# Convolution taps turned behind the first gate block, and block copies split by the partitions they write

## The chip, the cores and the metric

The kernel runs on one core of one Trainium2 chip. The metric is the device time of one launch in microseconds (us). Engines are named as the profile names them: PE is TensorE, DVE is VectorE, ACT is ScalarE, POOL is GpSimd, SP is SyncE.

## What is computed

An encoder trunk of two layers over 256 tokens of width 2048, in float32. Each layer is a token mixer followed by a gated MLP, with RMS normalisation in front and a residual add behind; the change touches only the MLP:

```python
def conv_ffn(h, w_up, conv_w, conv_b, w_down):
    u = h @ w_up                       # 2048 -> 2 * 5632
    u = conv over positions, width 3, one filter per channel (u, conv_w) + conv_b
    gate, val = jnp.split(u, 2, axis=-1)
    return (jax.nn.silu(gate) * val) @ w_down

for i in range(2):
    h = h + mixer_i(rms_norm(h, mix_norm[i]))
    h = h + conv_ffn(rms_norm(h, ffn_norm[i]), w_up[i], conv_w[i], conv_b[i], w_down[i])
return rms_norm(h, final_norm)
```

## The kernel before

Every large product is a stream of PE matmuls of 128x128 by 128x512. Weights arrive from HBM as `raw` tiles (128x1024 floats, half of a 512-row group) through SP's DMA queue, six buffers in turn. ACT rounds each to `wh` (line 126), DVE subtracts to get the rest `wl` (line 127), and PE multiplies three times: high by high, high by `wl`, low by high (lines 151 to 153). The pair `wh`, `wl` has three buffers in turn, so ACT begins a split when PE has left the buffers of three splits ago. One split feeds twelve matmuls. The two lines are built at a raised priority, so that the scheduler puts them ahead of other work in the queues of ACT and DVE; otherwise each engine does its instructions in one fixed order.

In the MLP the up-projection is done in 22 output blocks of 512 channels per layer, a gate block and its value block in turn (11 pairs, 6 in the first half and 5 in the second; behind each half stands its part of the down-projection, lines 259 to 264). A block is 96 matmuls, eight splits. When its sums are complete, the generator `up_post` is started, which goes on a step at a time while PE works on the next block:

- ACT scales the sums out of PSUM to `s` (line 426), and DVE transposes 32x32 squares from `s` to `t` (line 427). This turns the squares, but leaves them in the wrong partitions.
- Sixteen copies move them from `t` to `u`, each from 32 partitions to 32 partitions. Copy `i` reads partition group `a = i // 4` and writes group `b = (i // 4 + i) % 4`; within `u` the columns that different `a` write interleave. `PLACE` (line 26) names the engine of each: `p` POOL (line 436), `a` ACT (line 438), anything else DVE (line 440). Before, the sixteen letters go by `i`: five for POOL, three for ACT, eight for DVE, and every group `b` is written by several engines.
- ACT and DVE do the convolution with the taps `cw` (lines 446, 450, 452), ACT the silu (455), DVE the product with the value block (460 or 468), and both engines the split of the result for the down-projection (276, 277). Part of the down-projection uses seven products in place of eight, for which DVE also adds activations (484 to 496) and weights (line 228).

The framework adds semaphore waits between instructions that touch the same tile in overlapping places. It takes two copies to the same partitions with interleaving columns as overlapping.

The taps lie in HBM by row. Two DMAs on POOL's queue bring them to `cr` (lines 392, 393), and `taps()` turns them: three PE transposes into one PSUM bank (line 399) and a DVE copy to `cw` (line 400). `taps_gen` is started before the first block and runs when `step()` next reaches it, which is in the first splits of the first gate block. That block and its value block are done by `project2`: three of four row groups of the gate, three of the value, then `drain()`, the last group of the gate, `first_done` (which starts `up_post` of the gate), and the last group of the value.

In layer 0 there is one more piece of side work in the MLP, `bias_lines`: six PE products, each copied by DVE to one of two halves of `lnt` (line 890) and sent to HBM by four DMAs on POOL's queue (line 894).

Of the kernel before, what the change touches and what calls it, by code (L numbers as in the profile page):

```python
# [18 lines left out]
NPAIR = 11  # L19
# [3 lines left out]
NRAW, NHL = 6, 3  # L23
SKG = ((0, 2), (0,))
ORDER = (1, 2, 5, 3, 7, 6, 4)
PLACE = "pvavpvpvavpvpvav"
AHEAD = 45
NWARM = 11

# [2 lines left out]
def tile_encoder(ctx: ExitStack, tc: tile.TileContext, x, xT, w_a, w_ao, q_gain, k_gain, w_b, w_bo,  # L32
# [34 lines left out]
    def ps_tile():  # L67
        bank_at[1] = (bank_at[1] + 1) % 4
        return bank(4 + bank_at[1], "ps")
# [12 lines left out]
    def start(gen):  # L82
        if next(gen, StopIteration) is not StopIteration:
            pending.append(gen)
# [15 lines left out]
    def drain(keep=0):  # L100
        while len(pending) > keep:
            step()
# [34 lines left out]
    def feed(accs, lhs, kg, wap, first, last, by_m=False, pieces=2, mid=None):  # L137
        raws = [new_raw(), new_raw()]
        for i in range(pieces):
            w = 2048 // pieces  # L140
            r = raws[2 * i // pieces].rearrange("p a c -> p (a c)")
            o = i * w % 1024
            nc.sync.dma_start(r[:, o:o + w], wap[:, i * w:(i + 1) * w])
            if mid is not None:
                mid(i)
        def mms(order):
            for m, kt in order:
                (wh, wl), j = hls[kt // 2], kt % 2
                xh, xl = at(lhs[4 * kg + kt], m)
                st, sp = first and kt == 0, last and kt == 3  # L150
                nc.tensor.matmul(accs[m], xh, wh[:, j, :], start=st, stop=False)  # L151
                nc.tensor.matmul(accs[m], xh, wl[:, j, :], start=False, stop=False)  # L152
                nc.tensor.matmul(accs[m], xl, wh[:, j, :], start=False, stop=sp)  # L153

        hls = []
        for s in range(2):
            r = raws[s]
            if pieces == 4:
                wh, wl = new_hl()
                with tc.high_priority(offset=AHEAD):  # L160
                    for i in range(2):
                        nc.scalar.activation(wh[:, i], r[:, i], AF.Copy)  # L162
                        nc.vector.tensor_tensor(wl[:, i], r[:, i], wh[:, i].bitcast(F32), ALU.subtract)
                done_raw(r)
                hls.append((wh, wl))
            else:
                hls.append(split_raw(r))
            if not by_m:
                mms([(m, kt) for kt in (2 * s, 2 * s + 1) for m in range(2)])
                step()  # L170
        if by_m:
            mms([(m, kt) for m in range(2) for kt in range(4)])

    def new_acc():
        bank_at[0] = (bank_at[0] + 2) % 4
        return [bank(bank_at[0] + m, "acc") for m in range(2)]
# [8 lines left out]
    def project2(w, n0, n1, lhs, kgs, late, first_done, hook=None):  # L185
        a0, a1 = new_acc(), new_acc()
        early = len(kgs) - late
        for k, part in enumerate((range(early), range(early, len(kgs)))):
            if k == 1:
                drain()  # L190
            for accs, n in ((a0, n0), (a1, n1)):
                for i in part:
                    kg = kgs[i]
                    mid = hook and hook(n == n0, kg)
                    feed(accs, lhs, kg, w[n, kg], i == 0, i == len(kgs) - 1,
                         pieces=4 if hook and i < 2 else 2, mid=mid)
                if k == 1 and n == n0:
                    first_done(a0)
        return a1
# [182 lines left out]
    def ffn(l, hT, ss_in, g_next, last, side=None):  # L382
        with tc.tile_pool(name=nm("wpool"), bufs=1) as wp, tc.tile_pool(name=nm("fpool"), bufs=1) as fp:
# [11 lines left out]
            def taps():  # L395
                t = ps_tile()
                for a in range(3):
                    w = min(P, NROW - a * P)
                    nc.tensor.transpose(t[:, a * P:a * P + w], cr[:w, a, :], ident[:w, :w])
                nc.vector.tensor_copy(cw, t[:, :NROW])  # L400
# [6 lines left out]
            for u in us:  # L407
                nc.gpsimd.memset(u[:, :, P:P + 1], 0.0)

            def taps_gen():  # L410
                yield
                taps()

            start(taps_gen())

            def halves(v):
                return v.rearrange("p (m t) -> p m t", m=2)

            def up_post(acc, n, cs, after=None):
                u = us.pop(0)  # L420
                us.append(u)
                yield
                s = fp.tile([P, 2, 512], F32, tag="s", name=nm("s"))
                t = fp.tile([P, 2, 512], F32, tag="t", name=nm("t"))
                for m in range(2):
                    nc.scalar.activation(s[:, m], acc[m], AF.Copy, scale=rstd[:, m:m + 1])
                    nc.vector.transpose(t[:, m], s[:, m])  # L427
                yield
                tv = t.rearrange("p m (j q c) -> p j m q c", j=4, q=4)
                uv = u.rearrange("p j (m t) -> p j m t", m=2)  # L430
                for i in range(16):
                    a, b = i // 4, (i // 4 + i) % 4
                    dst = uv[32 * b:32 * b + 32, :, :, 32 * a:32 * a + 32]
                    src = tv[32 * a:32 * a + 32, :, :, b]
                    if PLACE[i] == "p":
                        nc.gpsimd.tensor_copy(dst, src)  # L436
                    elif PLACE[i] == "a":
                        nc.scalar.activation(dst, src, AF.Copy)  # L438
                    else:
                        nc.vector.tensor_copy(dst, src)  # L440
                yield
                for hh in range(2):
                    yield
                    c = cs[hh]
                    for j in range(2):
                        nc.scalar.activation(halves(c[:, j]), halves(u[:, 2 * hh + j])[:, :, :P], AF.Identity,
                                             bias=tap(n, 2 * hh + j, 3), scale=tap(n, 2 * hh + j, 1))
                    for j in range(2):
                        cj, uj = halves(c[:, j]), u[:, 2 * hh + j]
                        nc.vector.scalar_tensor_tensor(cj, halves(uj[:, :NT])[:, ::-1], tap(n, 2 * hh + j, 0), cj,  # L450
                                                       ALU.mult, ALU.add)
                        nc.vector.scalar_tensor_tensor(cj, halves(uj[:, 1:NT + 1])[:, ::-1], tap(n, 2 * hh + j, 2), cj,
                                                       ALU.mult, ALU.add)
                    if after is None:
                        nc.scalar.activation(c, c, AF.Silu)
                    else:
                        yield from after(hh)
# [43 lines left out]
            kgs = list(range(4))  # L501
            for hf, (p0, p1) in enumerate(HALVES):
# [8 lines left out]
                for p in range(p0, p1):  # L511
                    if p - p0 in SKG[hf]:
                        fm = forms[p - p0] = {f: new_form() for f in (1, 7, 2, 5, 4, 6, 3) + (0,) * hf}
                        if hf:
                            for kt in range(4):
                                slots[4 * (p - p0) + kt] = [
                                    tuple(t[:, kt % 2 * P:(kt % 2 + 1) * P] for t in fm[f])
                                    for f in ((1, 0), (2, 4))[kt // 2]]
                    else:
                        slots.update({4 * (p - p0) + j: new_form() for j in range(4)})  # L520
                    cg, cv = ([fp.tile([P, 2, NT], F32, tag=t, name=nm(t), bufs=3) for _ in range(2)]
                              for t in ("cg", "cv"))

                    def after(hh, cg=cg, cv=cv, slots=slots, forms=forms, kg=p - p0):
                        if kg in forms:
                            return glu_forms(cg[hh], cv[hh], forms[kg], hh)
                        return glu(cg[hh], cv[hh], slots, 4 * kg + 2 * hh)

                    if p == 0:
                        va = project2(w_up[l], p, NPAIR + p, hT, kgs, 1,  # L530
                                      lambda a, cg=cg: start(up_post(a, 0, cg)))
                    else:
                        start(up_post(project(w_up[l], p, hT, kgs), p, cg))
                        va = project(w_up[l], NPAIR + p, hT, kgs)
                    start(up_post(va, NPAIR + p, cv, after))
                    if p == 1 and side is not None:
                        spare.append(side(wp, fp))
# [491 lines left out]
    hT, ss = mixer_a()  # L1029
    hT, ss = ffn(0, hT, ss, 2, False, bias_lines)  # L1030
    hT, ss = mixer_b(hT, ss)
# [85 lines left out]
```

## Time and profile before

| | |
|---|---|
| median of 3 runs | 2297.68 us (2296.09 to 2298.33) |
| profiled execution, time | 2300.27 us |
| its span, first to last instruction | 2298.5 us |
| PE busy | 2263.6 us (98%) |
| DVE busy | 1808.1 us (79%) |
| ACT busy | 1296.6 us (56%) |
| POOL busy | 227.5 us (10%) |
| HBM traffic over the span | 189 GB/s |

A time in the trace is counted from the start of the span. A row of the timeline gives start, duration, engine, line, operation, and in brackets the idle time before it and what ended it. Matmuls overlap, each shown at about 0.39 us though the next begins sooner, so what PE loses is read from the distance between starts. Rows of several windows give for each stretch the busy time of each engine with its count, and the clock that PE was granted.

### The profile page before, as it was taken

What the parts mean: (1) busy time and instruction counts of PE and PEld (TensorE: products, weight loads), DVE (VectorE), ACT (ScalarE), POOL (GpSimd) and SP (SyncE); (2) the same over time, 40 slices, a digit from 0 to 9 for tenths busy, and PEclk for the clock granted to TensorE, in tenths of its full rate; (3) what the DMA queues carried; (4) which work ended last, traced back from release to release, by engine and by line L of the source; (5) the groups of instructions that cost most, each with busy time, mean ns of one, the idle gap of its engine ahead of it and who ended that gap; (6) DMA issues with size and microseconds to landing.
All of it is one profiled execution on the core that took longest, in us unless ns stands there. A gap on an engine that the chain in (4) does not pass through costs nothing.

```text
span 2298.5 us, 28788 instructions
## 1 busy us (share of the span) xinstructions
PE 2263.6 (98%) x10169; PEld 1863.5 (81%) x10169; DVE 1808.1 (79%) x2697; ACT 1296.6 (56%) x1846; POOL 227.5 (10%) x328
## 2 busy tenths in 40 slices
PE   9999899999999999999999999999999999999998
PEld 7788688787888888888888888877788878888876
DVE  6877778888978888978776876584988888788884
ACT  6565456666546666555554554454766655466653
POOL 2210012211001111010000000000211100111110
PEclk9999999999999999999999999999999999999999
DMA  8445557765666565666655565555556566656663
GB/s 300 151 144 156 177 168 210 224 196 170 217 209 189 191 197 163 214 223 196 197 177 171 181 191 164 177 185 191 184 191 193 187 200 209 192 184 196 208 209 128
DMA packets 126449, 437.42 MB, mean 190 GB/s; under 512 B 17264, under 2 KB 18032, under 8 KB 126304
## 3 DMA queue, kind: packets, MB, share of 16 engines
q1 hardware_dynamic: 119744, 425.64, 57.8%
q0 software_dynamic: 6128, 9.38, 1.6%
q8 instruction: 79, 1.29, 0.2%
q14 instruction: 66, 0.54, 0.1%
q10 hardware_dynamic: 432, 0.56, 0.1%
HBM read 429.20 MB, written 6.29 MB: 189 GB/s over the span
## 4 chain that ended last, share of the span: by engine, by line
PE 80%; DVE 13%; issue 3%; DMA 2%; ACT 1%; POOL 1%; SPq 0%; DVEq 0%; POOLq 0%; ACTq 0%
PE acc L152 21%; PE acc L153 21%; PE acc L151 21%; DVE wl L127 6%; PE acc L264 5%; PE acc L261 4%; PE acc L259 4%; DVE tT L320 1%; DVE u L440 1%; ACT wh L126 1%; DMA scr<-lnt 1%; DVE al L277 1%; DVE cv L450 1%; PE ps L291 1%; DVE t L427 1%
## 5 line engine op out<-in xcount | busy, mean ns | idle before, releaser
L127 DVE TENSOR_TENSOR wl<-raw,wh 128x1024 fp32r<-128x1024 f32 x822 | 1001.4, 1225 | 318.1 <-ACT wh L126 313.4
L126 ACT ACTIVATE wh<-raw 128x1024 fp32r<-128x1024 f32 x822 | 863.8, 1057 | 630.0 <-PE acc L153 403.8
L152 PE MATMUL acc<-wl,xh 128*128 128x512 f32 x2176 | 853.0, 392 | 6.3 <-DVE wl L127 5.5
L151 PE MATMUL acc<-wh,xh 128*128 128x512 f32 x2176 | 854.2, 393 | 0.1
L153 PE MATMUL acc<-wh,xh 128*128 128x512 f32 x2176 | 850.3, 391 | 0.0
L152 PEld LDWEIGHTS acc<-wl,xh 128*128 128x128 f32 x2176 | 409.8, 188 | 99.3 <-DVE wl L127 15.6
L153 PEld LDWEIGHTS acc<-wh,xh 128*128 128x128 f32 x2176 | 409.9, 188 | 84.4
L151 PEld LDWEIGHTS acc<-wh,xh 128*128 128x128 f32 x2176 | 409.8, 188 | 83.8 <-ACT wh L162 0.6
L436 POOL COPY u<-t 32x256 f32<-32x256 f32 x220 | 141.2, 642 | 1044.1 <-DVE t L427 1016.2
L259 PE MATMUL acc<-wh,ah 128*128 128x512 f32 x524 | 204.2, 390 | 0.0
L261 PE MATMUL acc<-wh,al 128*128 128x512 f32 x524 | 204.2, 390 | 0.0
L152 PE MATMUL acc<-wl,ah 128*128 128x512 f32 x480 | 188.2, 392 | 2.0 <-DVE wl L127 1.8
L151 PE MATMUL acc<-wh,ah 128*128 128x512 f32 x480 | 187.6, 391 | 0.0
L153 PE MATMUL acc<-wh,al 128*128 128x512 f32 x480 | 187.3, 390 | 0.0
L264 PE MATMUL acc<-wl,ah 128*128 128x512 f32 x524 | 147.0, 392 | 5.8 <-DVE wl L127 5.5
L440 DVE COPY u<-t 32x256 f32<-32x256 f32 x352 | 125.6, 357 | 15.7 <-ACT u L438 5.7
L264 PEld LDWEIGHTS acc<-wl,ah 128*128 128x128 f32 x524 | 97.6, 188 | 29.5 <-DVE wl L127 9.6
L259 PEld LDWEIGHTS acc<-wh,ah 128*128 128x128 f32 x524 | 98.5, 188 | 20.5
L261 PEld LDWEIGHTS acc<-wh,al 128*128 128x128 f32 x524 | 98.4, 188 | 20.5
L438 ACT ACTIVATE u<-t 32x256 f32<-32x256 f32 x132 | 55.2, 418 | 97.9 <-DVE u L440 85.6
L152 PEld LDWEIGHTS acc<-wl,ah 128*128 128x128 f32 x480 | 90.2, 188 | 23.9 <-DVE wl L127 5.8
L151 PEld LDWEIGHTS acc<-wh,ah 128*128 128x128 f32 x480 | 90.2, 188 | 18.3
(170 smaller groups left out, 1622.9 us busy)
## 6 DMA issues: line engine op xcount, KB each, us to landing
raw<-in_w_up_dram SPq DMA_DIRECT2D x352, 512.0 KB, 4.4
raw<-in_w_down_dram SPq DMA_DIRECT2D x176, 512.0 KB, 4.6
raw<-in_w_b_dram SPq DMA_DIRECT2D x144, 512.0 KB, 4.0
raw<-in_w_bo_dram SPq DMA_DIRECT2D x48, 512.0 KB, 4.0
raw<-in_w_a_dram SPq DMA_DIRECT2D x40, 512.0 KB, 4.8
raw<-in_w_ao_dram SPq DMA_DIRECT2D x32, 512.0 KB, 4.0
raw<-in_w_a_dram SPq DMA_DIRECT2D x16, 256.0 KB, 6.3
h<-in_x_dram SPq DMA_DIRECT2D x4, 512.0 KB, 9.1
```

What stands on the lines that cost most here:

```text
L126: nc.scalar.activation(wh, r, AF.Copy)
L127: nc.vector.tensor_tensor(wl, r, wh.bitcast(F32), ALU.subtract)
L151: nc.tensor.matmul(accs[m], xh, wh[:, j, :], start=st, stop=False)
L152: nc.tensor.matmul(accs[m], xh, wl[:, j, :], start=False, stop=False)
L153: nc.tensor.matmul(accs[m], xl, wh[:, j, :], start=False, stop=sp)
L259: nc.tensor.matmul(acc[k], xh, wh[:, j, :], start=k in fresh, stop=False)
L261: nc.tensor.matmul(acc[k], xl, wh[:, j, :], start=False, stop=False)
L264: nc.tensor.matmul(acc[k], xh, wl[:, j, :], start=False, stop=last[k] == i and j == 1)
L277: nc.vector.tensor_tensor(lo, src, hi.bitcast(F32), ALU.subtract)
L436: nc.gpsimd.tensor_copy(dst, src)
L438: nc.scalar.activation(dst, src, AF.Copy)
L440: nc.vector.tensor_copy(dst, src)
```

## The change

Two edits. First, `taps()` is no longer a generator of its own; it is called when the first gate block is complete, in front of that block's `up_post`. The two DMAs to `cr` stay where they were. Second, `PLACE` has four letters and is read by the written group `b`: group 0 is written by POOL, groups 1 and 3 by ACT, group 2 by DVE. So of the sixteen copies of a block POOL has four (five before), ACT eight (three) and DVE four (eight); there are 44 blocks in all.

```diff
-PLACE = "pvavpvpvavpvpvav"
+PLACE = "pava"
...
             for u in us:
                 nc.gpsimd.memset(u[:, :, P:P + 1], 0.0)
 
-            def taps_gen():
-                yield
-                taps()
-
-            start(taps_gen())
-
             def halves(v):
...
-                    if PLACE[i] == "p":
+                    if PLACE[b] == "p":
                         nc.gpsimd.tensor_copy(dst, src)
-                    elif PLACE[i] == "a":
+                    elif PLACE[b] == "a":
                         nc.scalar.activation(dst, src, AF.Copy)
                     else:
                         nc.vector.tensor_copy(dst, src)
...
                     if p == 0:
-                        va = project2(w_up[l], p, NPAIR + p, hT, kgs, 1,
-                                      lambda a, cg=cg: start(up_post(a, 0, cg)))
+                        def gate_done(a, cg=cg):
+                            taps()
+                            start(up_post(a, 0, cg))
+
+                        va = project2(w_up[l], p, NPAIR + p, hT, kgs, 1, gate_done)
```

Lines behind line 409 move up by six in the changed kernel, and lines behind line 531 by three, so the copies stand there at 430 (POOL), 432 (ACT) and 434 (DVE).

Nothing else moves on PE, and SP's order is unchanged. PE's queue in layer 0, at the second split of the first gate block, before (`acc_2629` is the gate's second half, `xh_2296` the last input slice of the first row group, `h` is transposed for later input slices):

```order
L151 MATMUL acc_2629<-wh_2657,xh_2296 128x512
L399 MATMUL ps_2652<-ident,cr_2603 128x128 x2
L152 MATMUL acc_2629<-wl_2658,xh_2296 128x512
L399 MATMUL ps_2652<-ident,cr_2603 128x96
L153 MATMUL acc_2629<-wh_2657,xh_2296 128x512
L347 MATMUL ps_2673<-ident,h 128x128 x4
```

The three transposes of the taps stood in the middle of a group of matmuls. After the change they stand behind the last matmul of the gate block, in front of the value block's last row group (`acc_2630`):

```order
L152 MATMUL acc_2629<-wl_2891,xh_2707 128x512
L153 MATMUL acc_2629<-wh_2890,xh_2707 128x512
L399 MATMUL ps_2906<-ident,cr_2603 128x128 x2
L399 MATMUL ps_2906<-ident,cr_2603 128x96
L151 MATMUL acc_2630<-wh_2915,xh_2673 128x512
L152 MATMUL acc_2630<-wl_2916,xh_2673 128x512
```

They moved by 146 matmuls; layer 1 has the same move.

ACT's queue for a block in the middle of layer 0, before, with the engines whose semaphores a row waits on (`t_4445` is the block's transposed tile, `u_2606` its destination):

```order
L426 ACTIVATE s_4444<-acc_4233,rstd_2597 128x512
L126 ACTIVATE wh_4502<-raw_4483 128x1024 [waits DMAHW2_49,DVE_49,PE_49]
L438 ACTIVATE u_2606<-t_4445 32x8x32 [waits DVE_49] x3
L126 ACTIVATE wh_4529<-raw_4525 128x1024 [waits DMAHW3_49,PE_49]
```

and after:

```order
L420 ACTIVATE s_4444<-acc_4233,rstd_2597 128x512
L126 ACTIVATE wh_4502<-raw_4483 128x1024 [waits DMAHW2_49,DVE_49,PE_49]
L432 ACTIVATE u_2606<-t_4445 32x8x32 [waits DVE_49]
L432 ACTIVATE u_2606<-t_4445 32x8x32
L432 ACTIVATE u_2606<-t_4445 32x8x32 [waits Activation_49] x4
L126 ACTIVATE wh_4529<-raw_4525 128x1024 [waits DMAHW3_49,PE_49]
L432 ACTIVATE u_2606<-t_4445 32x8x32 [waits Activation_49]
L432 ACTIVATE u_2606<-t_4445 32x8x32
```

Only the first copy waits for another engine, and six copies instead of three stand in front of the next weight split.

DVE's queue for the same block, before:

```order
L427 STREAM_TRANSPOSE t_4445<-s_4444 128x512 [waits Activation_49]
L440 COPY u_2606<-t_4445 32x8x32 [waits DVE_49]
L440 COPY u_2606<-t_4445 32x8x32
L440 COPY u_2606<-t_4445 32x8x32 [waits Pool_49] x3
L127 TENSOR_TENSOR wl_4503<-raw_4483,wh_4502 128x1024 [waits DMAHW2_49,Activation_49]
L440 COPY u_2606<-t_4445 32x8x32 [waits Activation_49]
L440 COPY u_2606<-t_4445 32x8x32 [waits Pool_49]
L440 COPY u_2606<-t_4445 32x8x32 [waits Activation_49]
```

and after:

```order
L421 STREAM_TRANSPOSE t_4445<-s_4444 128x512 [waits Activation_49]
L434 COPY u_2606<-t_4445 32x8x32 [waits DVE_49] x3
L127 TENSOR_TENSOR wl_4503<-raw_4483,wh_4502 128x1024 [waits DMAHW2_49,Activation_49]
L434 COPY u_2606<-t_4445 32x8x32 [waits DVE_49]
L127 TENSOR_TENSOR wl_4530<-raw_4525,wh_4529 128x1024 [waits DMAHW3_49,Activation_49]
```

DVE's copies no longer wait for POOL or ACT, and three instead of five stand in front of the next subtraction. Each copy waits for the copy before it on its own engine.

## The prediction

> **What bounds the kernel now.** I read the page first, then windows over the MLP, then PE's timeline where they show a loss, and last the queues of ACT and DVE. The page gives PE, and the copies by engine:
>
> ```profile
> PE 2263.6 (98%) x10169; PEld 1863.5 (81%) x10169; DVE 1808.1 (79%) x2697; ACT 1296.6 (56%) x1846; POOL 227.5 (10%) x328
> L436 POOL COPY u<-t 32x256 f32<-32x256 f32 x220 | 141.2, 642 | 1044.1 <-DVE t L427 1016.2
> L440 DVE COPY u<-t 32x256 f32<-32x256 f32 x352 | 125.6, 357 | 15.7 <-ACT u L438 5.7
> L438 ACT ACTIVATE u<-t 32x256 f32<-32x256 f32 x132 | 55.2, 418 | 97.9 <-DVE u L440 85.6
> ```
>
> PE is the bound almost everywhere, so a change off PE counts only where PE stands still. The windows (length, then busy us and count of PE, PEld, DVE, ACT, POOL, then PE's clock) say where that is:
>
> ```profile
> 279.00:286.00 7.00, 5.38 (x16) 4.38 (x17) 3.10 (x5) 1.90 (x3) 0.00 (x0) 0.52 0.27 95
> 316.00:372.00 56.00, 55.06 (x241) 44.56 (x240) 52.62 (x92) 41.31 (x62) 10.76 (x17) 1.00 0.60 185
> 372.00:428.00 56.00, 54.09 (x225) 42.94 (x224) 42.75 (x72) 30.75 (x46) 22.33 (x35) 0.97 0.77 232
> 428.00:550.00 122.00, 121.99 (x538) 100.76 (x537) 104.36 (x169) 79.31 (x116) 17.89 (x29) 1.00 0.64 200
> 550.00:583.00 33.00, 31.68 (x138) 25.50 (x138) 31.52 (x44) 20.71 (x28) 3.26 (x5) 1.00 0.48 152
> 905.00:930.00 25.00, 23.06 (x100) 18.06 (x99) 24.88 (x34) 15.90 (x22) 1.65 (x2) 1.00 0.52 175
> 1608.00:1665.00 57.00, 56.10 (x245) 45.42 (x244) 53.53 (x95) 42.01 (x63) 11.81 (x20) 1.00 0.60 185
> 1840.00:1870.00 30.00, 28.68 (x125) 23.03 (x124) 27.34 (x39) 18.08 (x24) 2.70 (x5) 1.00 0.56 188
> 2190.00:2215.00 25.00, 23.77 (x104) 18.98 (x104) 25.00 (x33) 15.37 (x20) 0.00 (x0) 1.00 0.66 203
> ```
>
> In the middle of an up-projection (428 to 550) PE is never idle: 122.00 / 538 = 0.227 us for each matmul, my pitch below. It is idle where the up-projection begins (316, 1608) and where the down-projection begins (550, 905, 1840, 2190), and there DVE is full: 31.52 of 33, 25.00 of 25. The largest loss is in front of these, in the first gate block. PE's timeline in layer 0, then layer 1, with the two DMA issues of layer 0 on POOL:
>
> ```profile
> 273.98 0.39 PE L151 MATMUL acc<-wh,xh 128*128 128x512 f32 x1
> 277.14 0.41 PE L399 MATMUL ps<-ident,cr 128*128 128x128 f32 x2 [2.77 <-POOL rb L877]
> 280.62 0.42 PE L399 MATMUL ps<-ident,cr 96*128 96x96 f32 x1 [2.83 <-DMA cr<-in_conv_dram]
> ...
> 285.58 0.47 PE L153 MATMUL acc<-wh,xh 128*128 128x512 f32 x1
> 285.89 0.39 PE L151 MATMUL acc<-wh,xh 128*128 128x512 f32 x1
> 1570.67 0.39 PE L151 MATMUL acc<-wh,xh 128*128 128x512 f32 x1
> 1573.51 0.41 PE L399 MATMUL ps<-ident,cr 128*128 128x128 f32 x2 [2.45 <-issue]
> 1574.98 0.60 PE L347 MATMUL ps<-ident,h 128*128 128x128 f32 x4
> 1575.34 0.48 PE L151 MATMUL acc<-wh,xh 128*128 128x512 f32 x1
> 1575.65 0.40 PE L152 MATMUL acc<-wl,xh 128*128 128x512 f32 x1
> 272.64 0.79 POOL L392 DMA_DIRECT2D cr<-in_conv_dram  x1 [94.07 <-DMA raw<-in_w_up_dram]
> 275.01 0.57 POOL L393 DMA_DIRECT2D cr<-in_conv_dram  x1
> ```
>
> The taps' transposes stand in PE's queue a microsecond or two behind the issue of the DMAs that feed them, and the whole queue waits for the landing, once for each DMA.
>
> **The taps.** Layer 0: from 273.98 to 285.89 are 11.91 us. Twelve 512-wide matmuls begin in it: 12 x 0.227 = 2.72. The four transposes of `h` cost 0.36 (1574.98 to 1575.34), and the matmul behind them 0.31 in place of 0.227: 0.44 together. So 8.75 us are lost, of which some 2 are no wait: behind it PE ran at clock 0.52 (window 279 to 286). Layer 1: from 1570.67 to 1575.65 are 4.98, less four matmuls (0.91) and 0.44: 3.63. At the new place the same three transposes cost three quarters of 0.44 again, 0.33 for each layer, and no wait: their DMAs were issued at 272.64 and 275.01, some 40 us before. DVE's copy to `cw` stands in front of one `wl`, where DVE has slack. Gain: 8.75 + 3.63 - 0.66 = 11.7. What is late next there? The late input slices that the four transposes of `h` feed are used only behind five sixths of both blocks, and the weights keep PE fed at 0.227 on both sides, so nothing; I take 11 to 12.
>
> [...]
>
> **Copies on ACT.** Five more for each of 44 blocks at 418 ns: 220 x 0.418 = 92 us more work. But an ACT copy now waits for DVE. The queue in mid-layer, ACT and then DVE:
>
> ```profile
> 488.69 0.42 ACT L438 ACTIVATE u<-t 32x256 f32<-32x256 f32 x1
> 489.49 0.42 ACT L438 ACTIVATE u<-t 32x256 f32<-32x256 f32 x1 [0.39 <-DVE u L440]
> 491.62 0.41 ACT L438 ACTIVATE u<-t 32x256 f32<-32x256 f32 x1 [1.71 <-DVE u L440]
> 492.06 1.06 ACT L126 ACTIVATE wh<-raw 128x1024 fp32r<-128x1024 f32 x1
> 487.86 2.05 DVE L440 COPY u<-t 32x256 f32<-32x256 f32 x5
> 489.94 1.23 DVE L127 TENSOR_TENSOR wl<-raw,wh 128x1024 fp32r<-128x1024 f32 x1
> 556.55 3.01 DVE L440 COPY u<-t 32x256 f32<-32x256 f32 x8
> ```
>
> The three copies hold ACT from 488.69 to 492.03, and `wh` waits behind them. Afterwards six copies at about 0.43 (0.44 from the last one's start to that of `wh`) stand there, 2.6 us, so that `wh` begins near 491.3, and two more follow it: eight copies take 3.4 us where three took 3.3. Over all blocks: 55.2 + 97.9 = 153 us before, 352 x 0.43 = 151 after. ACT's bill is level, its cover the waits that go; if the waits stayed, each `wh` would come 2 us later. POOL's four copies (4 x 0.642 = 2.6) end within ACT's eight.
>
> **Copies on DVE.** Four fewer for each block: 4 x 0.357 = 1.43 us (the eight in the last row, 3.01 us, give 1.5). Where PE never idles this is worth nothing. At the four starts of the down-projection DVE is full and PE waits for `wl`:
>
> ```profile
> 572.25 0.39 PE L261 MATMUL acc<-wh,al 128*128 128x512 f32 x1
> 573.87 1.21 PE L264 MATMUL acc<-wl,ah 128*128 128x512 f32 x4 [1.23 <-DVE wl L127]
> L264 PE MATMUL acc<-wl,ah 128*128 128x512 f32 x524 | 147.0, 392 | 5.8 <-DVE wl L127 5.5
> ```
>
> 573.87 - 572.25 - 0.227 = 1.39 us of loss, and the last block's copies stand in the full stretch before it. The four windows hold 1.32 + 1.94 + 1.32 + 1.23 = 5.8 us of idle PE (25 - 23.77 in the last), nearly the sum that the group's row puts to `wl`. Relief of 1.43 at each is at most 5.7; I take 5.5. It is 2 if ACT's extra copies make `wh` late there instead.
>
> [...]
>
> DVE's copies, and POOL's, now each wait for the one before on their own engine. No row shows that alone; the eight copies above have six waits in them and still run at 3.01 / 8 = 0.376, so I take nothing for it (0 to 0.1 us a copy, 0.4 a block, hidden except at the four starts).
>
> **The beginnings of the up-projection** (316, 1608: 0.94 and 0.90 us of idle PE). Two blocks end there 5.4 us apart, and ACT had little to wait for:
>
> ```profile
> 321.79 0.42 ACT L438 ACTIVATE u<-t 32x256 f32<-32x256 f32 x1 [0.38 <-DVE u L440]
> 323.92 0.42 ACT L438 ACTIVATE u<-t 32x256 f32<-32x256 f32 x1 [0.99 <-DVE u L440]
> 336.07 1.22 DVE L127 TENSOR_TENSOR wl<-raw,wh 128x1024 fp32r<-128x1024 f32 x1
> ```
>
> Ten more copies (4.3 us) against 1.4 of waits: `wh` comes up to 2.9 us later, DVE has eight copies (2.9) less. Going down the two new queues with these durations, the `wl` that began at 336.07 begins 0.4 later. I take a loss of 0.5 in each layer; ends: 0.9 gained and 2.9 lost. Other waits for `wl` are spread thinly:
>
> ```profile
> PE acc L152 <- DVE wl L127: 7.3, 13, 1.8
> ```
>
> Of these 7.3 us the three windows from 316, 372 and 1608 can hold 0.94 + 1.91 + 0.90 = 3.75. The other 3.5 lie in later blocks of the up-projection, which gain DVE's relief, and in the mixers, which don't; I take somewhat over half, 2.0, as gone (ends 0 and 3.5).
>
> **The side work of layer 0** (372 to 428, 1.91 us idle, clock 0.97) hangs on DMAs from `lnt`:
>
> ```profile
> 409.90 0.42 DVE L890 COPY lnt<-ps 128x256 f32<-128x256 f32 x1 [2.48 <-DMA scr<-lnt]
> ```
>
> This wait depends on POOL's DMAs, which move little. I take 0, ends -3 and +2.
>
> **Sum.** 11.7 + 5.5 + 2.0 - 1.0 = 18.2, less 0.7 for lateness of `wh` that I do not see: 17.5 off the profiled execution, 2300.27 to 2282.8. That execution lies 2.6 over the median, so **2280.2** is forecast against 2297.68.
>
> **Rivals.**
> - *Copies neutral.* ACT's added copies take at the starts what DVE is spared. Only the taps count: 11.7 off, 2286.0. For it: ACT's work rises by 92 us. Against: the level bill above.
> - *The taps' wait is replaced.* Without the pause the weight stream or input slices are late at the same place, and most of it is paid again; only the copies count, 6 off: 2291.7. Against: PE runs at pitch up to 273.98 and from 285.89 on.
> - *Slower: ACT becomes the bound.* A `wh` behind six copies in a row is late by more than the three buffers hide. A split lasts 12 x 0.227 = 2.72 us; three buffers give 5.4, less 1.06 + 1.23 for `wh` and `wl`: 3.1 of slack, of which the wait for `t` and 2.6 of copies can take all. The point is 11.7 / 44 = 0.27 us a block. At 0.6 us a block PE loses 26: 2297.7 + 26 - 11.7 = 2312. For it: six in a row is nearly one split. Against: 492.06 would move forward, not back.
>
> A measurement of this kernel can tell about 0.2% (4.6 us) from no change.
>
> **Chances.** The forecast 0.60, copies neutral 0.22, taps replaced 0.08, slower 0.10. The range takes the first three, with the ends of the unknown costs: down to 17.5 + 3 + 2.8 (all of the starts, the beginnings) = 23, 2275, a microsecond more for the small waits: 2274; up to the third case, 2292. Faster 0.86 (0.60, 0.22, and half of the third case, which lies near the edge at 2293.1), same 0.05 (the other half and 0.01 of the last), slower 0.09.
>
> **What would show it.** Right: no gap on PE in front of line 399, clock 1.00 from 274 to 291; no row of ACT waiting for DVE's copies, ACT's copies x352 at 0.42 with a few us idle; DVE's x176; PE's idle in front of `wl` in the four windows under 0.5 us each. Wrong: new gaps on PE in front of lines 151 or 152 in mid-layer windows where 121.99 of 122 were busy (ACT the bound), a gap near 280 put to a weight or an `xh` (taps replaced), or DVE's copies far over 0.4 us through their own waits.

## The result, and the profile after

| | before | after |
|---|---|---|
| median | 2296.89 us (2295.47 to 2305.48, 6 runs) | 2284.16 us (2283.76 to 2286.94, 6 runs) |
| ratio, 95% interval | | 0.9942 [0.9926, 0.9958] |
| profiled execution, its span | 2300.27 us, 2298.5 us | 2283.76 us, 2281.9 us |

The change saves 12.7 us, 0.6%. The forecast was 17.5 (2280.2 us); 2284.16 lies inside the range (2274 to 2292), and 1.8 us from the rival "copies neutral" (2286.0). The range held that rival and "taps replaced" too, so lying inside it says little about the copies. One of the eleven executions of the kernel that has only the new copies ran at a mean granted clock of 0.587 and took 3600 us; the ratios leave it out, and as it was the profiled one, that kernel has no trace that can be compared.

The page of the changed kernel, busy time by engine and the groups that answer to those shown before (the copies stand at lines 430 to 434 there):

```profile
PE 2256.4 (99%) x10169; PEld 1861.7 (82%) x10169; DVE 1756.7 (77%) x2521; ACT 1392.9 (61%) x2066; POOL 198.9 (9%) x284
L430 POOL COPY u<-t 32x256 f32<-32x256 f32 x176 | 112.9, 642 | 1056.8 <-DVE t L421 1048.6
L432 ACT ACTIVATE u<-t 32x256 f32<-32x256 f32 x352 | 147.7, 420 | 22.2 <-DVE t L421 14.4
L264 PE MATMUL acc<-wl,ah 128*128 128x512 f32 x524 | 147.0, 392 | 4.3 <-DVE wl L127 3.7
```

ACT's copies are 352, at 420 ns, and what they still wait for is the block's own transpose (14.4 of 22.2 us), no longer DVE's copies. PE's idle time in front of the down-projection's `wl` products fell only from 5.8 to 4.3 us. The windows of the changed kernel follow; from the third row on they are nearly the stretches of work shown before, each starting earlier by what had been saved by then:

```profile
274.00:279.00 5.00, 5.00 (x27) 4.16 (x26) 2.33 (x3) 2.56 (x4) 3.19 (x8) 1.00 0.83 234
279.00:286.00 7.00, 6.79 (x30) 5.26 (x29) 2.96 (x5) 1.75 (x4) 0.00 (x0) 1.00 0.47 174
308.70:364.70 56.00, 54.05 (x237) 43.70 (x236) 48.16 (x78) 46.62 (x76) 6.41 (x12) 1.00 0.59 181
364.70:417.70 53.00, 53.00 (x231) 43.10 (x230) 40.47 (x63) 38.20 (x62) 23.47 (x36) 1.00 0.82 251
417.70:539.30 121.60, 121.60 (x538) 100.75 (x537) 98.15 (x148) 90.87 (x142) 13.21 (x21) 1.00 0.64 200
539.30:572.30 33.00, 31.99 (x140) 25.76 (x139) 30.46 (x40) 22.57 (x33) 3.37 (x4) 1.00 0.50 153
892.20:917.20 25.00, 23.88 (x104) 19.07 (x103) 24.31 (x35) 17.76 (x25) 0.77 (x2) 1.00 0.59 184
1593.70:1649.70 56.00, 54.09 (x236) 43.72 (x235) 48.52 (x79) 46.97 (x77) 8.74 (x16) 1.00 0.60 183
1823.30:1853.30 30.00, 29.11 (x127) 23.41 (x126) 26.75 (x36) 20.49 (x30) 3.38 (x4) 1.00 0.57 192
2173.10:2198.10 25.00, 23.73 (x101) 18.57 (x101) 24.96 (x33) 16.47 (x22) 0.00 (x0) 1.00 0.61 198
```

Where the taps stood, PE is full but for 0.21 us and its clock is 1.00 (before: 1.01 of 5, and 5.38 of 7 at 0.52). The middle of the up-projection is full as before. The four starts of the down-projection (from 539.3, 892.2, 1823.3, 2173.1) hold 1.01 + 1.12 + 0.89 + 1.27 = 4.3 us of idle PE, 5.8 before. The two beginnings of the up-projection (308.7 and 1593.7) hold 1.95 and 1.91, 0.94 and 0.90 before. The side work (364.7 to 417.7) lost nothing in this execution; the profiled execution of before lost 1.91 us there and ran at a clock of 0.97 (the window from 372 in the prediction), which is one reason why the two profiled times lie 16.5 apart and the medians 12.7. Whether that comes from the change can't be told from one trace of each; with the old copies and the taps one row group earlier 0.82 us were lost there, at clock 1.00 (362 to 416).

### The profile page after: what moved, and what is told of

It reads as the page before. It is cut to its first block, busy times and chain, and to the rows that moved or that the text cites. A ratio compares the mean times of both kernels' runs of the same rounds, so it can differ in the third digit from the quotient of the medians.

```text
span 2281.9 us, 28779 instructions
## 1 busy us (share of the span) xinstructions
PE 2256.4 (99%) x10169; PEld 1861.7 (82%) x10169; DVE 1756.7 (77%) x2521; ACT 1392.9 (61%) x2066; POOL 198.9 (9%) x284
## 5 line engine op out<-in xcount | busy, mean ns | idle before, releaser
L430 POOL COPY u<-t 32x256 f32<-32x256 f32 x176 | 112.9, 642 | 1056.8 <-DVE t L421 1048.6
L432 ACT ACTIVATE u<-t 32x256 f32<-32x256 f32 x352 | 147.7, 420 | 22.2 <-DVE t L421 14.4
L261 PEld LDWEIGHTS acc<-wh,al 128*128 128x128 f32 x524 | 98.5, 188 | 20.5
L153 PEld LDWEIGHTS acc<-wh,al 128*128 128x128 f32 x480 | 90.2, 188 | 18.2
```

Of the source, the lines that this page charges most:

```text
L261: nc.tensor.matmul(acc[k], xl, wh[:, j, :], start=False, stop=False)
```

## Experiments

All were run five rounds beside the kernel before. "Saved" is the difference of medians inside one comparison.

| taps | old copies (16 letters) | new copies `pava` | `pavv` |
|---|---|---|---|
| old place, waiting for their DMAs | 0 | 1.7 | |
| behind the gate block (the change) | 7.5 | **12.7** | 19.3 |
| one row group earlier | 12.1 | 12.1 | 18.6 |

**The taps alone.** The new place of the taps with the sixteen letters of before.

```diff
-            start(taps_gen())
...
+                        def gate_done(a, cg=cg):
+                            taps()
+                            start(up_post(a, 0, cg))
```

> The taps turned behind the first gate block, the block copies as before. My theory (the taps are worth 11.7 us by the wait for their DMAs, the rest of the change some 1 to 2): 11 to 12 us under before, about 2285.2. Rival 'the taps' wait is replaced' (weights or input slices late at the same place): under 6 off, 2291 or more. Rival 'the copies carry the gain': under 4 off.

Measured: 2290.16 us against 2297.7, ratio 0.9970 [0.9959, 0.9982]; 5 us less was saved than expected, and more than either rival allows. The pause is gone (in layer 0 ACT begins to scale the first gate block at 308.54 us, before at 316.57), but a new gap stands at the first pair of blocks. PE's timeline there:

```profile
325.66 0.39 PE L151 MATMUL acc<-wh,xh 128*128 128x512 f32 x1
328.52 0.50 PE L152 MATMUL acc<-wl,xh 128*128 128x512 f32 x1 [2.47 <-DVE wl L127]
```

The starts are 2.86 us apart, 2.63 more than the pitch; the same gap stands in layer 1 (1610.55 to 1613.42). DVE's queue in front of the late `wl`:

```profile
309.26 0.71 DVE L421 STREAM_TRANSPOSE t<-s 128x512 f32<-128x512 f32 x1 [0.50 <-ACT s L420]
309.89 0.49 DVE L400 COPY cw<-ps 128x352 f32<-128x352 f32 x1
...
321.48 1.21 DVE L127 TENSOR_TENSOR wl<-raw,wh 128x1024 fp32r<-128x1024 f32 x1
322.73 1.73 DVE L434 COPY u<-t 32x256 f32<-32x256 f32 x5
324.49 0.70 DVE L444 SCALAR_TENSOR_TENSOR cg<-u,cw,cg 128x256 f32<-128x256 f32 x1
...
326.85 0.48 DVE L446 SCALAR_TENSOR_TENSOR cg<-u,cw,cg 128x256 f32<-128x256 f32 x1
327.25 2.35 DVE L127 TENSOR_TENSOR wl<-raw,wh 128x1024 fp32r<-128x1024 f32 x2
```

The copy to `cw` now stands among the first block's post-processing, and further on 4.6 us of copies and convolutions lie between two `wl`s.

**The copies alone.** The letters of the change, the taps at their old place.

```diff
-PLACE = "pvavpvpvavpvpvav"
+PLACE = "pava"
...
-                    if PLACE[i] == "p":
+                    if PLACE[b] == "p":
```

> The block copies by written partitions, the taps as before. My theory (DVE's relief at the starts of the down-projection is mostly spent on weight splits that stand behind eight ACT copies in a row, and the first blocks lose some 1.5 us in each layer): 0 to 3 us under before, 2294 to 2297, with the two waits of PE in front of the taps unchanged. As predicted on record (5.5 + 2.0 - 1.0 - 0.7): 5.8 off, 2291. Rival 'ACT becomes the bound': slower than before.

Measured: 2296.04 us against 2297.7, ratio 0.9994 [0.9985, 1.0003]: no difference that can be told from none, and at most some 3.4 us saved. With the taps at their old place the forecast's 5.8 us are excluded.

**The old place without the wait.** The taps turned where they were, from the tile `ones`, which is ready long before, in place of `cr`. The kernel leaves out the right taps, and so doesn't compute the layer.

```diff
-                    nc.tensor.transpose(t[:, a * P:a * P + w], cr[:w, a, :], ident[:w, :w])
+                    nc.tensor.transpose(t[:, a * P:a * P + w], ones[:w, :], ident[:w, :w])
```

> Before, with the taps turned at their old place, but from the constant tile of ones in place of the tile that the two DMAs fill; the DMAs stay, the convolution has wrong taps. If the loss is the wait for the DMAs' landing, it goes here as well: 11 to 12 us under before, clock 1.00 behind the transposes, no gap in front of line 399. If it is the place itself (three transposes in the middle of a group, a PSUM bank, the switch of operand type): within 2 us of before.

Measured: 2285.83 us against 2297.7, ratio 0.9946 [0.9932, 0.9960], 11.9 saved. The same transposes at the same place cost nothing once they don't wait for the DMAs: the wait and the clock of 0.52 behind it are the whole loss. The windows that held the pause:

```profile
274.00:279.00 5.00, 5.00 (x26) 4.04 (x25) 2.79 (x3) 1.71 (x3) 3.63 (x9) 1.00 0.85 236
279.00:286.00 7.00, 7.00 (x33) 5.58 (x32) 2.48 (x4) 1.96 (x4) 0.00 (x0) 1.00 0.49 175
```

**Old copies, taps one row group earlier.** `taps` is handed to `project2` as `ahead`, so it is called 24 matmuls before the gate block is complete; the letters are those of before.

```diff
             if k == 1:
                 drain()
+                if ahead is not None:
+                    ahead()
```

> The copies are those of before (16 letters). The taps are turned one row group earlier than in the change: behind the drain, ahead of the gate block's last row group, some 24 matmuls (5.4 us) before the gate block is complete and still some 30 us behind their DMAs. Theory: taps alone came to 2290.2 instead of 2286 because DVE's copy to the taps stands there between the gate block's transpose and its sixteen copies, and with it the first convolutions fall into another gap between two weight splits on DVE, so that one split is late by 2.9 us in each layer. With the taps ready 5 us sooner that queue is as it was before: 2290.2 - 2 x 2.9 = 2284.4 (2283 to 2286). Rival: the 2.9 us belong to the first two blocks once the pause is gone, whatever stands in front of the gate's copies: 2290 as with the taps alone.

Measured: 2285.99 us against 2298.13, ratio 0.9946 [0.9934, 0.9959], 12.1 saved, as the theory had it. DVE's queue at the same place (two lines more in this kernel, so copies at 436, convolution at 446 and 448):

```profile
320.99 1.21 DVE L127 TENSOR_TENSOR wl<-raw,wh 128x1024 fp32r<-128x1024 f32 x1
322.13 0.47 DVE L448 SCALAR_TENSOR_TENSOR cg<-u,cw,cg 128x256 f32<-128x256 f32 x1
322.63 2.18 DVE L436 COPY u<-t 32x256 f32<-32x256 f32 x6
324.84 1.23 DVE L127 TENSOR_TENSOR wl<-raw,wh 128x1024 fp32r<-128x1024 f32 x1
```

From the end of one `wl` to the next are now 2.6 us, not 4.6. A copy of half a microsecond cost some 4.2 us by where it fell in the order (2290.16 against 2285.99; the intervals of the two ratios just touch). The three transposes on PE moved with it.

**The change's copies, taps one row group earlier.** The last kernel with the other edit of the change:

```diff
-PLACE = "pvavpvpvavpvpvav"
+PLACE = "pava"
...
-                    if PLACE[i] == "p":
+                    if PLACE[b] == "p":
```

> The copies of the change (POOL 4, ACT 8, DVE 4, each group of partitions written by one engine), the taps one row group earlier, where with the old copies 2286.0 us was measured. The difference of the two is what the change's copies are worth when the taps' copy doesn't stand in front of them. Theory: the copies gain the small waits in mid-layer (3 us) and 1.5 us at the four starts of the down-projection, and pay ACT's longer row twice at the beginnings of the up-projection (1 us each): 2286.0 - 2.5 = 2283.5 (2282 to 2285). Rival: the 6 us between the change and the taps alone (2284.2 against 2290.2) are all the copies' worth: 2280.

Measured: 2284.55 us against 2296.7, ratio 0.9944 [0.9930, 0.9957]; with the old copies it was 0.9946. The rival (copies worth 6) falls; the result lies in the theory's range, a microsecond above its 2283.5. Here and with the taps at their old place the change's copies are worth 0 to 1.7 us. The windows show why, old copies first (starts of the down-projection, then a beginning of the up-projection):

```profile
538.00:571.00 33.00, 31.61 (x138) 25.50 (x137) 30.20 (x42) 20.47 (x28) 3.25 (x5) 1.00 0.43 143
1590.00:1646.00 56.00, 55.06 (x241) 44.52 (x240) 51.08 (x88) 39.95 (x61) 9.85 (x15) 1.00 0.53 179
```

and with the copies of the change:

```profile
538.00:571.00 33.00, 32.37 (x142) 26.10 (x141) 30.33 (x39) 22.81 (x33) 3.37 (x4) 1.00 0.45 151
1590.00:1646.00 56.00, 54.04 (x235) 43.60 (x234) 47.96 (x77) 46.50 (x75) 7.24 (x12) 1.00 0.55 181
```

At the start 0.76 us is gained, at the beginning 1.0 is lost. All four starts hold 5.6 us of idle PE with the old copies and 3.7 with the new, the two beginnings 1.9 and 3.9: what is gained at the one is lost at the other.

**Eight copies on DVE, four on ACT.** The change with one letter different: group 3 goes from ACT to DVE.

```diff
-PLACE = "pava"
+PLACE = "pavv"
```

> The changed kernel with groups 2 and 3 both written by DVE (POOL 4, ACT 4, DVE 8): no copy waits for another engine, but DVE has its eight as before. If the later weight splits behind ACT's eight copies are what eats the relief: the wait of PE in the first blocks falls back to about 0.9 us in each window or less, at the starts of the down-projection PE waits about as before (5 to 6 us in the four), time within 1.5 us of the changed kernel. If DVE's relief is what counts: 3 to 6 us slower than the changed kernel.

Measured: 2278.44 us against 2297.7, ratio 0.9916 [0.9902, 0.9929]: 5.7 us faster than the change, though DVE has as many copies as before. Neither expectation had that. So sparing DVE four copies is worth less than giving them to ACT costs. The group of DVE's copies, and two starts of the down-projection with a beginning of the up-projection:

```profile
L434 DVE COPY u<-t 32x256 f32<-32x256 f32 x352 | 122.1, 347 | 11.1
538.00:571.00 33.00, 32.16 (x141) 25.95 (x140) 31.98 (x44) 21.02 (x29) 2.50 (x4) 1.00 0.47 155
891.00:916.00 25.00, 24.49 (x107) 19.59 (x106) 25.00 (x33) 16.17 (x21) 0.00 (x0) 1.00 0.60 184
1590.00:1646.00 56.00, 54.67 (x242) 44.89 (x241) 53.06 (x95) 43.04 (x66) 8.06 (x16) 1.00 0.57 184
```

DVE is as full at the starts as it ever was (31.98 of 33, 25.00 of 25), and PE is idle there 0.84 and 0.51 us, less than in the change (1.01 and 1.12). POOL's four copies, the same ones as in the change, are shorter here too (466 ns on average, 642 there); this run doesn't separate what that adds.

**The same with the taps one row group earlier.**

```diff
                         def gate_done(a, cg=cg):
-                            taps()
                             start(up_post(a, 0, cg))
...
-                        va = project2(w_up[l], p, NPAIR + p, hT, kgs, 1, gate_done)
+                        va = project2(w_up[l], p, NPAIR + p, hT, kgs, 1, gate_done, ahead=taps)
```

> As the last kernel with POOL 4, ACT 4 and DVE 8 copies (2278.4 us), but the taps are turned one row group earlier, so that DVE's copy to the taps (0.49 us) leaves the chain behind the first gate block. Theory: the loss of 1.5 us that is left in each layer at the first pair of blocks (PE gap 1.72 at 326 and at 1606) shrinks by the 0.5 us of that copy or by all of it if the order of DVE's queue returns to the one of before: 2275.5 to 2277.5. Rival: that loss comes from two blocks 5.4 us apart and not from the taps: 2278.4, same.

Measured: 2279.57 us against 2298.13, ratio 0.9920 [0.9907, 0.9934], the same as the last; the forecast of a gain is a miss. The rival's "same" came. PE's idle time at the beginning of the up-projection in layer 0 (306 to 362) shrank from 1.33 to 0.88 us, but the four starts hold 3.7 us of it, 2.9 with the taps at the change's place.

**The same numbers of copies, waits left in.** The sixteen letters of before with one `p` made `a`, so POOL 4, ACT 4, DVE 8 as in the last two, but every group is written by several engines; taps one row group earlier.

```diff
-PLACE = "pvavpvpvavpvpvav"
+PLACE = "pvavpvpvavpvavav"
```

> The sixteen letters of before with one POOL copy given to ACT: POOL 4, ACT 4, DVE 8, the same numbers as in the kernel of 2279.6 us, the taps at the same earlier place as there; only which engine writes which partitions differs (here every group is written by several engines, so copies wait across engines). Theory (the waits between engines count, not the numbers): 2286 as with the old letters (2284.5 to 2288), ACT idle some 100 us in front of its copies. Rival (the numbers count: one copy less on POOL): 2279.6.

Measured: 2285.74 us against 2296.7, ratio 0.9949 [0.9935, 0.9963]: like the old letters (0.9946), and not like `pavv` at the same place of the taps (0.9920). ACT's group, first here, then in the `pavv` kernel with the same taps:

```profile
L434 ACT ACTIVATE u<-t 32x256 f32<-32x256 f32 x176 | 73.6, 418 | 82.7 <-DVE u L436 69.6 <-DVE t L423 10.7
```

```profile
L434 ACT ACTIVATE u<-t 32x256 f32<-32x256 f32 x176 | 73.9, 420 | 11.9 <-DVE t L423 6.8
```

Same count, same duration; 70 us of waiting for DVE's copies are gone, and the kernel is some 6 us faster. This is what one writer for each group is worth here, with intervals of the two ratios that only just don't meet. Where the 6 us lie isn't shown: at the six places the two traces differ by 1.2 us of idle PE, and this kernel's trace lost 2.44 us in the side work at a clock of 0.97, the other 0.48 at 1.00 (362 to 416).

**All sixteen on ACT.** Taps as in the change.

```diff
-PLACE = "pava"
+PLACE = "aaaa"
```

> The change with all sixteen copies on ACT: none crosses to another engine, DVE and POOL have none. ACT's copies 704 x 0.42 = 296 us instead of 148; in most blocks nine and seven copies stand in front of two splits one behind the other. Theory (ACT's row of copies costs once it is longer than the slack of three buffers, 3.1 us): two splits are 5.4 us of PE, ACT has 2 x 1.06 + 16 x 0.43 + 0.68 = 9.7 us to do in them, 5.4 + 3.1 = 8.5 are free, so 1.2 us a block are lost in mid-layer too, 44 x 1.2 = 53 us: 2337 (2315 to 2365). Rival (ACT's copies count only at the six places where two blocks or a down-projection follow closely): eight more copies, 3.4 us, at six places: 2305 at most, and no gap on PE in mid-layer.

Measured: 2361.63 us against 2298.13, ratio 1.0278 [1.0261, 1.0295]: the theory's range held it, at its upper end; the rival falls. Nine and seven copies stand in front of two splits in mid-layer; ACT's queue and PE:

```profile
500.59 3.92 ACT L432 ACTIVATE u<-t 32x256 f32<-32x256 f32 x9
504.54 1.06 ACT L126 ACTIVATE wh<-raw 128x1024 fp32r<-128x1024 f32 x1
506.91 0.50 PE L152 MATMUL acc<-wl,xh 128*128 128x512 f32 x1 [0.76 <-DVE wl L127]
417.70:539.30 121.60, 117.43 (x502) 94.46 (x501) 81.63 (x118) 99.71 (x173) 0.00 (x0) 0.99 0.54 181
```

The mid-layer window carries 502 matmuls where it carried 538: 36 x 0.226 = 8.1 us lost in 5.6 blocks of 96, 1.5 a block; 4.17 us of it are shown as idle PE, and the clock in the window was 0.99. So the prediction's slower rival is real as a mechanism; its point lies somewhere between the change's rows of six, which lost nothing in mid-layer, and nine and seven.

**None on ACT.** Taps as in the change.

```diff
-PLACE = "pava"
+PLACE = "pvpv"
```

> The change with POOL and DVE eight copies each and ACT none; no copy waits for another engine's copy. Theory (what the change gains is the waits between engines, and what it gives back are ACT's copies in front of the weight splits): with none on ACT at least as good as with four (2278.4): 2276 to 2278.5, and the gaps at the starts of the down-projection smaller. Rival (POOL, 0.47 to 0.64 us a copy, becomes the chain: 8 x 0.55 = 4.4 us against DVE's 2.9, so the convolutions begin 1.5 us later): 2280 to 2286, with the gaps at the first pair and at the starts of the down-projection larger by up to 1.5 each.

Measured: 2288.81 us against 2298.13, ratio 0.9961 [0.9948, 0.9973]: worse than both expectations, and 10 us worse than `pavv`. The copies on POOL and DVE, and a gap at the first pair of blocks:

```profile
L430 POOL COPY u<-t 32x256 f32<-32x256 f32 x352 | 182.8, 519 | 996.5 <-DVE t L421 978.5
L434 DVE COPY u<-t 32x256 f32<-32x256 f32 x352 | 139.0, 395 | 11.1
320.81 4.71 POOL L430 COPY u<-t 32x256 f32<-32x256 f32 x8 [3.74 <-DVE t L421]
328.41 0.50 PE L152 MATMUL acc<-wl,xh 128*128 128x512 f32 x1 [1.90 <-DVE wl L127]
```

POOL needs 4.7 us for this block (4.2 on average), and DVE's copies take 395 ns in place of 347. PE's idle time in front of the down-projection's `wl` products is 6.9 us, 4.3 in the change, and in front of the `wl` products on line 152 (those with `xh`) 9.7, 6.5 in the change. Which of the two engines makes these losses wasn't separated.

## Why the prediction was right, and where its sizes were off

**The taps: right in size.** 11.7 us were forecast for the wait; three kernels without it saved 11.9 (old place, no wait), 12.1 (earlier place, old copies) and 12.1 (earlier place, new copies). That the landing is the cause, and not the place, is shown by the first. In the changed kernel the matmuls that took 11.91 us in layer 0 take 3.20:

```profile
274.24 0.39 PE L151 MATMUL acc<-wh,xh 128*128 128x512 f32 x1
277.44 0.39 PE L151 MATMUL acc<-wh,xh 128*128 128x512 f32 x1
```

So 8.7 us went there, and in layer 1, in the same way, 3.6, where 8.75 and 3.63 were forecast; the transposes at their new place cost about the 0.33 each that was set against it. "Nothing is late next" held at that place but for 0.21 us (6.79 of 7 busy). The clock of 1.00 came as expected.

The lower clock behind the stall, by the prediction's estimate some 2 of the 8.75 us, doesn't go by a stall's length alone. In the taps-alone kernel a gap of 2.86 us between starts stands in layer 0 and one of 2.87 in layer 1: the 3.5 us behind it ran at clock 1.00 in layer 0, and the 3.4 us at 0.55 in layer 1 (rows below). In the kernel before, a gap of 2.20 us in the side work (409.32 to 411.52) was followed by a clock of 0.57 (412 to 416), and the one of 2.84 us in front of the taps of layer 1 (1570.67 to 1573.51) by 1.00 (1575.3 to 1578.8). So a stall much shorter than layer 0's can be paid for twice as well, and what decides it wasn't shown.

```profile
328.50:332.00 3.50, 3.48 (x15) 2.86 (x16) 3.50 (x7) 3.03 (x5) 0.00 (x0) 1.00 0.55 185
1613.40:1616.80 3.40, 3.38 (x9) 2.65 (x10) 3.40 (x7) 2.41 (x4) 0.00 (x0) 0.55 0.61 181
```

**"DVE's copy to `cw` stands in front of one `wl`, where DVE has slack": wrong as a general statement.** With the old copies it cost some 4.2 us (2290.16 against 2285.99 when the copy comes 5 us earlier). With the change's copies it cost nothing that can be measured (2284.16 and 2284.55). That is also why the two halves of the change saved 7.5 and 1.7 us alone and 12.7 together: the new copies do little by themselves, but with them the late `cw` no longer hurts. Why it doesn't is argued, not tested: in the changed kernel DVE waits 2.74 us for `wh` at that pair of blocks (row below), which leaves room for a copy of 0.49.

**The copies: 5.8 us were forecast (5.5 + 2.0 - 1.0 - 0.7), 0 to 1.7 measured.** This is the mis-sized term. Added to the taps alone the copies do bring 5.2 us (12.7 against 7.5), but most of that is the cost of the late `cw` that they take away, which the forecast had at nothing, and not the gains that it listed. At the places that it named the traces show 1.5 us gained and 2.0 lost:
- *The starts of the down-projection*, 5.5 forecast, 5.8 - 4.3 = 1.5 found. The failing step is "relief of 1.43 at each": DVE's freed time was taken as passed on in full to the `wl` that PE waits for. (Even then 1.43 at most, in windows with 1.32, 1.94, 1.32 and 1.23 us of idle PE, comes to 5.3 and not 5.5.) DVE had four copies fewer and then waited for ACT. ACT's and DVE's queues at the first start in the changed kernel:

```profile
544.92 3.52 ACT L432 ACTIVATE u<-t 32x256 f32<-32x256 f32 x8 [2.40 <-DVE t L421]
548.47 2.01 ACT L126 ACTIVATE wh<-raw 128x1024 fp32r<-128x1024 f32 x2
547.83 1.15 DVE L434 COPY u<-t 32x256 f32<-32x256 f32 x3
549.57 2.36 DVE L127 TENSOR_TENSOR wl<-raw,wh 128x1024 fp32r<-128x1024 f32 x2 [0.58 <-ACT wh L126]
```

  Eight copies stand in one row in front of `wh`; before, one copy stood in front of the first `wh` here and two in front of the next. All four starts have the same row of eight, 3.52 us, and the same wait of DVE behind it, 0.58 or 0.59 us. That is 0.6 of the 1.43; where the rest of the missing relief went wasn't read. The prediction's "2 if ACT's extra copies make `wh` late there instead" was the end that came. No window fell under the 0.5 us of idle PE that the forecast asked for. With four copies on ACT and eight on DVE these starts were better.
- *The beginnings of the up-projection*, a loss of 0.5 each forecast, 1.0 each found (1.95 and 1.91 idle against 0.94 and 0.90), by the mechanism named: rows of seven and six copies on ACT, and DVE idle behind them.

```profile
314.15 3.08 ACT L432 ACTIVATE u<-t 32x256 f32<-32x256 f32 x7
317.25 1.06 ACT L126 ACTIVATE wh<-raw 128x1024 fp32r<-128x1024 f32 x1
318.34 1.23 DVE L127 TENSOR_TENSOR wl<-raw,wh 128x1024 fp32r<-128x1024 f32 x1 [2.74 <-ACT wh L126]
```

- *ACT's level bill.* 153 us before; 151 forecast, 147.7 + 22.2 = 170 found. Closer than "92 us more", and mid-layer it cost nothing (121.60 of 121.60 us busy). But a bill over all blocks says nothing on the six places that count: there the copies that came stand in a row in front of `wh`.
- *The small waits*, 2.0 forecast, none found. The changed kernel's waits of the up-projection and the mixers for `wl`, in us, times and longest:

```profile
PE acc L152 <- DVE wl L127: 7.8, 15, 1.1
```

  Before they were 7.3, of which 3.5 lay outside the beginnings and the side work; now 3.9 of the 7.8 do. The rows show no relief there. The 0.7 for lateness of `wh` had no row behind it; the lateness that came is in the entries on the starts and the beginnings.

**The rivals.** "Copies neutral" describes the result better than the forecast: its reason, that ACT's added copies take at the starts what DVE is spared, is in part what the rows show, and the loss at the beginnings takes the rest. It had been given 0.22. "The taps' wait replaced" didn't happen in the change. In the taps-alone kernel a part of it did (4.2 us), at another place than the one named.

**A better version.** `pavv` with the taps at the change's place: 2278.44 us, ratio 0.9916 [0.9902, 0.9929], faster than both kernels. Of its 5.7 us over the change, the idle PE at the four starts and the two beginnings accounts for 2.6 (4.3 against 2.9, and 3.9 against 2.7). The rest isn't located.

## What to carry to other kernels

That an engine is full in a window doesn't show what relieving it is worth: look at what stands in a row in front of the producer that it waits for, and move work only where that row isn't lengthened. When several engines write interleaved pieces of one tile, let each partition range have one writer; here that was worth some 6 us at equal numbers of copies. Two edits that were priced apart met in one engine's order (a copy of 0.49 us cost 4.2 us or nothing), so an edit that moves an instruction into a post-processing chain is priced by that queue's order at the place, not by its duration.

## What the runs showed of the hardware

POOL copies of the same size (32 x 256 floats) took 642 ns on average in the change, 466 in the `pavv` kernel and 519 with eight of them a block; in the change the shortest took 0.39 us, the longest 1.31. DVE's copies took 347 ns on average in `pavv`, 357 in the change and 395 with none on ACT; in the change the shortest took 0.28 us, the longest 0.44. In the change and in `pavv` POOL does the very same copies, and only the engine of another group differs, so a copy's time goes with what the other engines do. Which instruction slows it was not separated.

In the taps-alone kernel a gap of 2.87 us between the starts of two matmuls was followed by 3.4 us at clock 0.55 in layer 1, and one of 2.86 us by 3.5 us at clock 1.00 in layer 0.
